# Fewer, larger transfers in a two-mixer attention layer: both heads' spills in one, doubled loads from one source pattern, one buffer for the mixed values

## The chip, the cores and the metric

The kernel runs on one NeuronCore of a Trainium2 chip, in one launch. The metric is the device time in microseconds (us) of that core, as a median over runs; lower is better. The core's engines are TensorE (PE, with its weight loads as PEld), VectorE (DVE), ScalarE (ACT), GpSimd (POOL) and SyncE (SP). In this kernel SP issues every transfer between HBM and on-chip memory, one after the other, and 16 DMA engines carry them.

## The reference

The layer normalises `x` (2048 x 1024), projects it to queries, keys, values and gates of two mixers, runs both attentions, gates and projects back.

```python
hdn = rmsnorm(x, norm_gain[i])
proj = jnp.einsum("bsd,de->bse", hdn, w_in[i])
q_a, k_a, v_a, g_a, q_b, k_b, v_b, g_b = jnp.split(proj, split_at, axis=-1)
...
o_a, _, _ = banded_attention(q_a, k_a, v_a, A_WINDOW - 1, sinks=sinks_a[i])
o_a = o_a.reshape(b, S, A_WIDTH).astype(x.dtype) * jax.nn.silu(g_a)
...
o_b = dilated_attention(q_b, k_b, v_b)
o_b = o_b.reshape(b, S, B_WIDTH).astype(x.dtype) * jax.nn.silu(g_b)

mixed = jnp.concatenate([o_a, o_b], axis=-1)
x = x + jnp.einsum("bse,ed->bsd", mixed, w_out[i])
```

Mixer A is a sliding window of 128 tokens with grouped queries and sinks. Mixer B attends under three patterns, (window, dilation) = (128, 1), (512, 4) and (2048, 16), and merges the three outputs by their softmax denominators. Both have 8 heads of 64.

## The kernel before

**Stages.** `STAGES` lists eight: four "B" stages of two heads of mixer B each, two "A" stages of four query heads each, and two "O" stages that multiply by the halves of the output matrix. A stage has four slots (`sb`, 512 tokens each), a slot two halves (`hf`, 256 tokens). All products with weights are made of three float32r products each (`mm3`, L285 to L288), where weights and `x` are split in a high and a low part. `x` is split once, in stage 0, and stored in `xd`; later stages load the stored parts (`x_load`, L180), and the O stages load the mixed values from `mx` (L185).

**Mixer B.** In slot `sb` of a B stage the windowed pattern runs from on-chip data (`units_B`). Queries, keys, the keys' low parts, values, gates, the windowed output and its row statistics are spilled to HBM under the names `qd`, `kd`, `ld`, `vd`, `gd`, `od`, `sd` (`finish`, L405 to L418; L364 for `vd`; `units_B`, L833 and L836). Four units `units_D(si, r)`, one for each residue of the token number modulo 4, then do the dilated patterns: the first when its stage ends, the other three in the slots of the next stage. For each of its two heads a unit loads queries `cq`, keys `ck`, low key parts `cl` and values `cv` (L856 to L864). Keys have 64 rows and fill 128 partitions, so `ck` and `cl` come as two copies of the same 64 rows. The unit ends in `after` (L928): it loads the windowed statistics `s1c` once a stage, works out two sets of factors, writes them to HBM as `rD` and reads them back spread over 64 partitions each (`Rb`, in `bcast`, L957). POOL multiplies by the first set (L974), then by the second (L978), and the sum goes to `mx` (L987).

**Mixer A.** `units_A` ends in the same way with reciprocals `rA` (L740), a spread load `Rb` (L750), a product on POOL (L756) and a store to `mx` (L760).

**The order of work.** The kernel's code interleaves the projection of a slot with attention pieces by a cost account (`advance`), and a scheduler then fixes each engine's order before the program runs. SP runs its transfers in that fixed order. A transfer whose data or buffer isn't ready holds up all that stand behind it. Eight semaphores are shared in turn by the transfers, so a transfer can also wait for the one eight places ahead. `Rb` has one buffer, as have `o1c` and `gc`.

Of the kernel before, what the change touches and what calls it, by code (L numbers as in the profile page):

```python
# [18 lines left out]
KC = DM // 128  # L19
# [15 lines left out]
def hybrid_layer(ctx, tc, xT, xn, x, wB, wA, wO, ng, gains, sinks, rot, masks, ident, out):  # L35
# [54 lines left out]

    rs_row = [dram([256], f"rsr{hf}") for hf in range(8)]
    xd = [dram([128, 4, 1024], f"xd{hf}") for hf in range(8)]
    mx = [dram([128, KC, 256], f"mx{hf}") for hf in range(8)]

    def bcast_row(d, lo, n, parts=128):
        return bass.AP(tensor=d.tensor, offset=d.offset + lo, ap=[[0, parts], [1, n]])
# [175 lines left out]
    def spill_tiles(si):  # L272
        if si not in spill:
            spill[si] = {
                "q": dram([2, 4, 128, 512], f"qd{si}"),
                "k": dram([2, 4, 64, 512], f"kd{si}"),
                "l": dram([4, 128, 512], f"ld{si}"),
                "v": dram([4, 4, 128, 256], f"vd{si}"),
                "g": dram([4, 128, 512], f"gd{si}"),
                "o": dram([4, 128, 512], f"od{si}"),  # L280
                "s": dram([4, 32, 4, 4, 4], f"sd{si}"),
            }
        return spill[si]

# [106 lines left out]
    def finish(si, sb, half, t1s):  # L391
        kind = STAGES[si][0]
        KK, KL = K[si, sb]
        nk = 1 if kind == "A" else 2
        if half == 0 and sb > 0:
            pk, pl = K[si, sb - 1]
            for h in range(nk):
                nc.scalar.activation(KK[:, h, :, 0, :], f32(pk[:, h, :, 4, :]), AF.Copy)
            for h in range(2):
                hs = slice(64 * h, 64 * h + 64)  # L400
                nc.scalar.activation(KL[hs, h, :, 0, :], f32(pl[hs, h, :, 4, :]), AF.Copy)
        yield from qk_transposes(si, sb, half, t1s)
        if half == 0:
            return
        if kind == "B":  # L405
            d = spill_tiles(si)
            cs = slice(sb * 128, sb * 128 + 128)
            for h in range(2):
                nc.sync.dma_start(d["q"][h][:, :, cs].rearrange("r p c -> p r c"),
                                  f32(Q[si, sb][1][:, h]))  # L410
                nc.sync.dma_start(d["k"][h][:, :, cs].rearrange("r p c -> p r c"),
                                  f32(KK[:64, h, :, 1:5, :]).rearrange("p r i u -> p r (i u)"))
            for h in range(2):
                hs = slice(64 * h, 64 * h + 64)
                nc.sync.dma_start(d["l"][:, hs, cs].rearrange("r p c -> p r c"),
                                  f32(KL[hs, h, :, 1:5, :]).rearrange("p r i u -> p r (i u)"))
            nc.sync.dma_start(d["g"][:, :, cs].rearrange("r p c -> p r c"),
                              G[si, sb][0].rearrange("p r i u -> p r (i u)"))  # L418
            pending.extend(units_B(si, sb))
            if sb == 3:  # L420
                pending.extend(units_D(si, 0))
        else:
            pending.extend(units_A(si, sb))
# [297 lines left out]
    def units_A(si, sb):  # L721
        idx = STAGES[si][1]
        sc = wk.tile([128, 2, 4, 4], F32, name="scA")
        units = []
        osum = {}

        def rows(p):
            e = wk.tile([128, 2, 4], F32, name="eA")
            hs = slice(2 * p, 2 * p + 2)
            nc.vector.tensor_tensor(e, sc[:, 0, hs], sk[:, 4 * idx + 2 * p:4 * idx + 2 * p + 2, None].to_broadcast([128, 2, 4]),  # L730
                                    op=OP.add)
            nc.scalar.activation(e, e, AF.Exp)
            nc.vector.tensor_tensor(e, e, sc[:, 1, hs], op=OP.add)
            nc.vector.reciprocal(e, e)
            pr = ps.tile([8, 128], F32, name="po", bufs=2)
            nc.tensor.transpose(pr, e.rearrange("p h i -> p (h i)"), idf)
            rr = wk.tile([16, 128], F32, name="rr")
            nc.scalar.activation(rr[:8], pr, AF.Copy)
            d = dram([8, 128], f"rA{si}_{sb}_{p}")
            nc.sync.dma_start(d, rr[:8])  # L740
            osum["d", p] = d

        def final(p):
            t = osum[p]

            def load():
                d = osum["d", p]
                rb = osum["r", p] = wk.tile([128, 512], F32, name="Rb", bufs=1)
                for a in range(2):
                    nc.sync.dma_start(rb[64 * a:64 * a + 64, :],  # L750
                                      bass.AP(tensor=d.tensor, offset=d.offset + a * 512, ap=[[0, 64], [1, 512]]))
                nc.gpsimd.tensor_tensor(t, t, G[si, sb][p].rearrange("p r i u -> p (r i u)"), op=OP.mult)

            def scale():
                mix = osum["m", p] = wk.tile([128, 512], F32, name="o1c", bufs=1)
                nc.gpsimd.tensor_tensor(cm_view(mix), cm_view(t), to_cm(osum["r", p]), op=OP.mult)  # L756

            def store():
                for a in range(2):
                    nc.sync.dma_start(mx[2 * sb + a][:, 2 * idx + p, :], osum["m", p][:, 256 * a:256 * a + 256])  # L760
                osum_free()

            late.append([[1, load], [4, scale], [2, store]])

        for p in range(2):
            units.extend(pair_units(si, sb, p, sc, osum, rows, final))
        return units
# [55 lines left out]
    def units_B(si, sb):  # L823
        sc = wk.tile([128, 4, 2, 2], F32, name="scB")
        osum = osum_tile()
        d = spill_tiles(si)
        units = []
        for h in range(2):
            def after(h=h):
                if h == 1:  # L830
                    with nc.allow_non_contiguous_dma(reason="row statistics"):
                        for r in range(4):
                            nc.sync.dma_start(d["s"][:, :, sb, r, :].rearrange("i u k -> u i k"),  # L833
                                              sc[32 * r:32 * r + 32].rearrange("p i a h -> p i (a h)"))
                    cs = slice(sb * 128, sb * 128 + 128)
                    nc.sync.dma_start(d["o"][:, :, cs].rearrange("r p c -> p r c"), osum.rearrange("p (r c) -> p r c", r=4))  # L836
                    osum_free()
            stats = ([sc[:, i, 0, h:h + 1] for i in range(4)], [sc[:, i, 1, h:h + 1] for i in range(4)])
            units.append(window_unit(si, sb, h, stats, cm_view(osum[64 * h:64 * h + 64, :]), after))
        return units  # L840


    S1 = {}

    def units_D(si, r):
        d = spill_tiles(si)
# [3 lines left out]
        def dil(h):  # L850
# [3 lines left out]
            def load():  # L854
                q = wk.tile([128, 512], F32R, name="cq")
                nc.sync.dma_start(f32(q), d["q"][h, r])  # L856
                k = wk.tile([128, 512], F32R, name="ck")
                for a in range(2):
                    nc.sync.dma_start(f32(k[64 * a:64 * a + 64, :]), d["k"][h, r])
                kl = wk.tile([128, 512], F32R, name="cl")  # L860
                for a in range(2):
                    nc.sync.dma_start(f32(kl[64 * a:64 * a + 64, :]), d["l"][r, hp:hp + 64, :])
                v = wk.tile([128, 4, 128], F32R, name="cv")
                nc.sync.dma_start(f32(v), d["v"][r][:, :, 128 * h:128 * h + 128].rearrange("t p e -> p t e"))  # L864
                s["v"], s["q"], s["k"], s["kl"] = v, q, k, kl
# [62 lines left out]
            def after():  # L928
                if h == 0:
                    return  # L930
                if (si) not in S1:
                    t = wk.tile([128, 4, 4, 4], F32, name="s1c")
                    nc.sync.dma_start(t.rearrange("p s r k -> p (s r k)"), d["s"].rearrange("i u s r k -> (i u) (s r k)"))
                    S1[si] = t
                s1 = S1[si]
                A = s1[:, :, r, :].rearrange("p t (k h) -> p k h t", k=2)
# [19 lines left out]
                o2 = c["o2"]  # L956
                def bcast(k):  # L957
                    rb = wk.tile([128, 512], F32, name="Rb", bufs=1)
                    for a in range(2):
                        nc.sync.dma_start(rb[64 * a:64 * a + 64],  # L960
                                          bass.AP(tensor=dd.tensor, offset=dd.offset + 1024 * k + a * 512, ap=[[0, 64], [1, 512]]))
                    return rb

                rbs = []
# [18 lines left out]

                def store():
                    ch = 4 + STAGES[si][1]
                    for t_ in range(4):
                        nc.sync.dma_start(mx[2 * t_ + r // 2][:, ch, 128 * (r % 2):128 * (r % 2) + 128],  # L987
                                          o2[:, 128 * t_:128 * t_ + 128])
                    osum_free()

                late.append([[1, first], [4, second], [4, third], [1, fourth], [2, store]])
# [126 lines left out]
```

## Time and profile before

| | us |
|---|---|
| median of 3 runs | 1258.38 |
| lowest, highest of them | 1250.45, 1262.69 |
| the profiled execution, its own time | 1263.84 |
| its span, first to last instruction | 1262.1 |

The profile is of one execution. Its span lacks 1.7 us of that execution's time, and that time is 5.5 us above the median. By when the stages' transfers are issued, the four B stages take roughly the first 670 us (the first about 165), the A stages the time to about 1050 us, and the O stages the rest. The loads of the dilated units run from 181 us to 817 us, their `Rb` loads from 228 us to 879 us. In the profile, issuing a transfer isn't counted as busy time; DMA shares are the mean over the 16 engines, so one engine that has more than the others is not seen in them.

### The profile page before, as it was taken

How to read it: one execution, taken by the hardware profiler on the slowest of the kernel's cores; microseconds unless marked ns; L12 is line 12 of the kernel's file. 1: busy time of each engine (PE TensorE's matmuls, PEld its weight loads, DVE VectorE, ACT ScalarE, POOL GpSimd, SP SyncE). 2: the span in 40 equal slices, each digit the busy share in tenths (PEclk: the TensorE clock that was granted, in tenths of full speed). 3: DMA queues.
4: the chain of work that ended last, by engine and by line, in shares of the span. 5: the costliest groups of instructions: out<-in, count | busy, mean ns of one | idle time of the engine just before them, and what ended most of it. 6: DMA issues, size and time to landing. Idle time of an engine off the chain costs nothing.

```text
span 1262.1 us, 24533 instructions
## 1 busy us (share of the span) xinstructions
PE 1157.7 (92%) x8040; PEld 1126.5 (89%) x8040; DVE 770.7 (61%) x2228; ACT 760.8 (60%) x2103; POOL 600.2 (48%) x720
## 2 busy tenths in 40 slices
PE   6889999979888988889797999999999999999999
PEld 5889898879887987889797989998999999999998
DVE  6856664746745665656565758878767767622321
ACT  6577755757755755757566656877766667522220
POOL 3987642544431543623534545754755465333222
PEclk9899899989989998999898999999999999999999
DMA  8978899888887797899868877857635345455652
GB/s 266 316 229 266 270 301 279 219 258 260 258 256 219 234 275 213 258 268 266 256 192 256 253 236 216 242 153 218 203 125 170 120 137 165 157 183 189 204 192 84
DMA packets 213007, 279.66 MB, mean 222 GB/s; under 512 B 36104, under 2 KB 145424, under 8 KB 212880
## 3 DMA queue, kind: packets, MB, share of 16 engines
q1 hardware_dynamic: 212880, 278.10, 71.7%
q8 instruction: 64, 1.05, 0.3%
q14 instruction: 63, 0.52, 0.1%
HBM read 206.38 MB, written 71.64 MB: 220 GB/s over the span
## 4 chain that ended last, share of the span: by engine, by line
PE 48%; DMA 22%; ACT 8%; POOL 7%; DVE 7%; SPq 4%; issue 3%; POOLq 0%; DVEq 0%; ACTq 0%
PE pj L288 33%; DMA x<-xd 4%; DMA Rb<-rD 3%; DMA stg<-in_wB 2%; PE po L923 2%; PE po L808 2%; PE pt L792 2%; PE sc L655 2%; PE po L710 2%; PE sc L656 1%; DMA cl<-ld 1%; DMA x<-in_xT 1%; DMA stg<-in_wA 1%; DMA TT<-tab 1%; DMA x<-mx 1%
## 5 line engine op out<-in xcount | busy, mean ns | idle before, releaser
L288 PE MATMUL pj<-wh,x 128*128 128x384 f32 (+1 forms) x2016 | 560.4, 333 | 7.1 <-ACT wh L104 6.7
L288 PEld LDWEIGHTS pj<-wh,x 128*128 128x128 f32 x2016 | 378.3, 193 | 10.7 <-ACT wh L104 7.0
L288 PE MATMUL pj<-wl,x 128*128 128x384 f32 (+1 forms) x1008 | 333.2, 331 | 0.0
L288 PE MATMUL pj<-x,wgh 128*128 128x256 f32 x992 | 203.3, 295 | 2.4 <-DVE V L360 2.0
L288 PEld LDWEIGHTS pj<-wl,x 128*128 128x128 f32 x1008 | 195.4, 194 | 2.1 <-DVE wl L102 0.2
L288 PEld LDWEIGHTS pj<-x,wgh 128*128 128x128 f32 x992 | 164.5, 198 | 4.4 <-ACT V L475 2.6
L639 DVE TENSOR_TENSOR ptl<-pt,pth 128x512 fp32r<-128x512 f32 (+3 forms) x232 | 141.2, 619 | 42.9 <-ACT pth L638 41.1
L288 PE MATMUL pj<-x,wgl 128*128 128x256 f32 x496 | 145.4, 293 | 0.0
L638 ACT ACTIVATE pth<-pt 128x512 fp32r<-128x512 f32 (+3 forms) x232 | 121.5, 540 | 31.3 <-PE pt L909 10.5
L193 ACT ACTIVATE x<-x 128x512 fp32r<-128x512 f32 x92 | 55.7, 625 | 132.2 <-DMA x<-mx 67.8
L288 PE MATMUL pj<-wgh,x 128*128 128x256 f32 x496 | 131.0, 285 | 0.0
L195 POOL TENSOR_TENSOR x<-x 128x512 fp32r<-128x512 f32 x58 | 76.2, 1326 | 106.0 <-ACT x L193 98.2
L523 POOL TENSOR_TENSOR Q<-ob,Q 64x256 fp32r<-64x256 f32 x96 | 72.2, 752 | 91.3 <-ACT Q L522 85.1
L888 ACT ACTIVATE P<-P,scD 128x256 f32<-128x256 f32 (+3 forms) x128 | 71.6, 560 | 44.7 <-DVE scD L887 42.6
L288 PEld LDWEIGHTS pj<-x,wgl 128*128 128x128 f32 x496 | 98.3, 198 | 0.3
L288 PEld LDWEIGHTS pj<-wgh,x 128*128 128x128 f32 x496 | 95.3, 192 | 0.0
L477 DVE TENSOR_REDUCE un<-sq 128x4 f32<-128x256 f32 (+1 forms) x96 | 42.0, 438 | 77.5 <-ACT sq L474 73.8
L887 DVE CUSTOM_DVE_ANT_0 P<-sc,mk 128x256 f32<-128x256 f32 (+3 forms) x128 | 61.4, 485 | 44.4 <-PE sc L883 40.6
L226 POOL TENSOR_TENSOR fac<-un,mhalf 128x8 f32<-128x8 f32 (+1 forms) x48 | 84.7, 1764 | 3.0
L664 ACT ACTIVATE P<-P,scB 128x256 f32<-128x256 f32 (+1 forms) x128 | 63.0, 493 | 20.7 <-DVE scB L663 20.2
L501 POOL TENSOR_TENSOR un<-un,eps 128x8 f32<-128x8 f32 (+1 forms) x48 | 10.7, 223 | 133.7 <-DVE un L477 131.7
L974 POOL TENSOR_TENSOR o1c<-o1c,Rb 128x512 f32<-128x512 f32 x16 | 21.1, 1318 | 111.7 <-DMA Rb<-rD 72.3
(171 smaller groups left out, 2735.0 us busy)
## 6 DMA issues: line engine op xcount, KB each, us to landing
x<-xd SPq DMA_DIRECT2D x160, 512.0 KB
xd<-x SPq DMA_DIRECT2D x32, 512.0 KB
x<-mx SPq DMA_DIRECT2D x32, 512.0 KB
vd<-V SPq DMA_DIRECT2D x64, 128.0 KB
qd<-qc SPq DMA_DIRECT2D x32, 256.0 KB
TT<-tab SPq DMA_DIRECT2D x32, 256.0 KB
cv<-vd SPq DMA_DIRECT2D x32, 256.0 KB
ck<-kd SPq DMA_DIRECT2D x64, 128.0 KB
```

What stands on the lines that cost most here:

```text
L193: nc.scalar.activation(h, f, AF.Copy)
L195: eng.tensor_tensor(l, f, f32(h), op=OP.subtract)
L226: nc.gpsimd.tensor_tensor(y, u, mhalf.to_broadcast([128, n]), op=OP.pow)
L288: nc.tensor.matmul(o, a, b, start=first and n == 0, stop=last and n == 2, skip_group_check=True)
L477: nc.vector.tensor_reduce(uv, sq[:, :n].rearrange("p (h d) -> p h d", d=64), axis=AX.X, op=OP.add)
L523: nc.gpsimd.tensor_tensor(o[b], src[a], f32(o[a]), op=OP.subtract)
L638: nc.scalar.activation(hi, pt, AF.Copy)
L639: nc.vector.tensor_tensor(lo, pt, f32(hi), op=OP.subtract)
L655: nc.tensor.matmul(sc[:, j, :], q[h // 2][:, h % 2, i, :], kw, start=True, stop=False)
L664: nc.scalar.activation(pd, pd, AF.Exp, bias=nb[i], scale=-1.0, accum_out=l[i])
L887: nc.vector.tensor_tensor_reduce(pd, o[:, :m], m2[:, 512 - m:], -0.125, BIG, OP.add, OP.min, nb)
L888: nc.scalar.activation(pd, pd, AF.Exp, bias=nb, scale=-1.0, accum_out=l)
```

## The change

Ten places join transfers that moved neighbouring or repeated data.

- `qd` and `kd`: both heads in one store each.
- `ck` and `cl`: one load whose source repeats the 64 rows through a leading step of 0 with a count of 2 (`twice`).
- `Rb` in both mixers: one load whose source has the two halves as a leading dimension of 2, and the repetition over 64 partitions behind it.
- `sd`: the statistics are stored as they lie in `sc`, 16 values a partition, and rearranged when they are loaded, in four loads.
- `mx`: one HBM buffer in place of eight, so that the four stores of a dilated unit, and the two of a mixer A pair, become one each.

```diff
-    mx = [dram([128, KC, 256], f"mx{hf}") for hf in range(8)]
+    mx = dram([8, 128, KC, 256], "mx")
...
-                "s": dram([4, 32, 4, 4, 4], f"sd{si}"),
+                "s": dram([4, 128, 16], f"sd{si}"),
...
-            for h in range(2):
-                nc.sync.dma_start(d["q"][h][:, :, cs].rearrange("r p c -> p r c"),
-                                  f32(Q[si, sb][1][:, h]))
-                nc.sync.dma_start(d["k"][h][:, :, cs].rearrange("r p c -> p r c"),
-                                  f32(KK[:64, h, :, 1:5, :]).rearrange("p r i u -> p r (i u)"))
+            nc.sync.dma_start(d["q"][:, :, :, cs].rearrange("h r p c -> p (h r) c"),
+                              f32(Q[si, sb][1]).rearrange("p h r c -> p (h r) c"))
+            nc.sync.dma_start(d["k"][:, :, :, cs].rearrange("h r p c -> p (h r) c"),
+                              f32(KK[:64, :, :, 1:5, :]).rearrange("p h r i u -> p (h r) (i u)"))
...
-                for a in range(2):
-                    nc.sync.dma_start(rb[64 * a:64 * a + 64, :],
-                                      bass.AP(tensor=d.tensor, offset=d.offset + a * 512, ap=[[0, 64], [1, 512]]))
+                nc.sync.dma_start(rb, bass.AP(tensor=d.tensor, offset=d.offset, ap=[[512, 2], [0, 64], [1, 512]]))
...
-                for a in range(2):
-                    nc.sync.dma_start(mx[2 * sb + a][:, 2 * idx + p, :], osum["m", p][:, 256 * a:256 * a + 256])
+                nc.sync.dma_start(mx[2 * sb:2 * sb + 2, :, 2 * idx + p, :].rearrange("a p n -> p a n"),
+                                  osum["m", p].rearrange("p (a n) -> p a n", a=2))
...
-                        for r in range(4):
-                            nc.sync.dma_start(d["s"][:, :, sb, r, :].rearrange("i u k -> u i k"),
-                                              sc[32 * r:32 * r + 32].rearrange("p i a h -> p i (a h)"))
+                        nc.sync.dma_start(d["s"][sb], sc.rearrange("p i a h -> p (i a h)"))
...
+    def twice(dst, src):
+        nc.sync.dma_start(dst, bass.AP(tensor=src.tensor, offset=src.offset, ap=[[0, 2]] + [list(x) for x in src.ap]))
...
-                for a in range(2):
-                    nc.sync.dma_start(f32(k[64 * a:64 * a + 64, :]), d["k"][h, r])
+                twice(f32(k), d["k"][h, r])
...
-                for a in range(2):
-                    nc.sync.dma_start(f32(kl[64 * a:64 * a + 64, :]), d["l"][r, hp:hp + 64, :])
+                twice(f32(kl), d["l"][r, hp:hp + 64, :])
...
-                    nc.sync.dma_start(t.rearrange("p s r k -> p (s r k)"), d["s"].rearrange("i u s r k -> (i u) (s r k)"))
+                    ds = d["s"]
+                    with nc.allow_non_contiguous_dma(reason="row statistics"):
+                        for i in range(4):
+                            nc.sync.dma_start(t[32 * i:32 * i + 32].rearrange("u s r k -> u (s r) k"),
+                                              bass.AP(tensor=ds.tensor, offset=ds.offset + 4 * i,
+                                                      ap=[[16, 32], [512, 16], [1, 4]]))
...
-                    for a in range(2):
-                        nc.sync.dma_start(rb[64 * a:64 * a + 64],
-                                          bass.AP(tensor=dd.tensor, offset=dd.offset + 1024 * k + a * 512, ap=[[0, 64], [1, 512]]))
+                    nc.sync.dma_start(rb, bass.AP(tensor=dd.tensor, offset=dd.offset + 1024 * k, ap=[[512, 2], [0, 64], [1, 512]]))
...
-                    for t_ in range(4):
-                        nc.sync.dma_start(mx[2 * t_ + r // 2][:, ch, 128 * (r % 2):128 * (r % 2) + 128],
-                                          o2[:, 128 * t_:128 * t_ + 128])
+                    nc.sync.dma_start(mx[r // 2::2, :, ch, 128 * (r % 2):128 * (r % 2) + 128].rearrange("t p n -> p t n"),
+                                      o2.rearrange("p (t n) -> p t n", t=4))
```

The scheduler makes its order anew, so transfers also change places. SP shows it best. The first place is in stage 1, from the factors of the second dilated unit of stage 0 (`rD_1`) to the loads of the next unit. A row has the line, the two names with the program's numbers, the shape and a count. Before, on SP:

```order
L960 DMA Rb<-rD_1_3047 64x512 x2
L864 DMA cv<-vd_351 128x4x128
L364 DMA vd_2097<-V 4x32x256
L833 DMA sd_2100<-scB 32x4x4 x3
L364 DMA vd_2097<-V 4x32x256
L180 DMA x<-xd_106 128x1024 x4
L455 DMA TT<-tab_6_1405 128x512
L263 DMA RB<-rsr_98 128x256
L960 DMA Rb<-rD_1_3047 64x512 x2
L856 DMA cq<-qd_348 128x512
L859 DMA ck<-kd_349 64x512 x2
L862 DMA cl<-ld_350 64x512 x2
```

The same place in the changed kernel, on SP:

```order
L960 DMA Rb<-rD_1_3011 128x1x512
L364 DMA vd_2078<-V 4x32x256
L180 DMA x<-xd_106 128x1024 x3
L841 DMA ck<-kd_342 128x1x512
L180 DMA x<-xd_106 128x1024
L854 DMA cq<-qd_341 128x512
L263 DMA RB<-rsr_98 128x256
L841 DMA cl<-ld_343 128x1x512
L960 DMA Rb<-rD_1_3011 128x1x512
L841 DMA ck<-kd_342 128x1x512
```

Each pair of `64x512` loads has become one of `128x1x512`, and the loads `ck` and `cl` of the next head now stand between the unit's two `Rb` loads.

The second place, some rows later, is the store of that unit to `mx` and the factors of the third unit. Before, on SP:

```order
L987 DMA mx_108<-osum 128x128
L987 DMA mx_110<-osum 128x128
L987 DMA mx_112<-osum 128x128
L987 DMA mx_114<-osum 128x128
L180 DMA x<-xd_107 128x1024 x2
L955 DMA rD_2_3599<-rr 16x128
L180 DMA x<-xd_107 128x1024 x2
```

The same place in the changed kernel, on SP:

```order
L985 DMA mx<-osum 128x4x128
L180 DMA x<-xd_107 128x1024 x4
L969 DMA gc<-gd_345 128x512
L263 DMA RB<-rsr_99 128x256
L416 DMA gd_2079<-G 128x4x128
L956 DMA rD_2_3546<-rr 16x128
L829 DMA sd_2081<-scB 128x16
```

Four stores have become one, as have the four of the statistics, and the factors' store `rD_2` now stands behind all four loads of `x` rather than between them.

## The prediction

> **What bounds the kernel now.** I read the page first: busy shares, the DMA rows and the chain that ended last.
>
> ```profile
> span 1262.1 us, 24533 instructions
> ...
> PE 1157.7 (92%) x8040; PEld 1126.5 (89%) x8040; DVE 770.7 (61%) x2228; ACT 760.8 (60%) x2103; POOL 600.2 (48%) x720
> ...
> DMA packets 213007, 279.66 MB, mean 222 GB/s; under 512 B 36104, under 2 KB 145424, under 8 KB 212880
> q1 hardware_dynamic: 212880, 278.10, 71.7%
> ...
> PE 48%; DMA 22%; ACT 8%; POOL 7%; DVE 7%; SPq 4%; issue 3%; POOLq 0%; DVEq 0%; ACTq 0%
> ```
>
> PE is busy 92% of the span, and the 16 DMA engines 71.7% on average. SP's issuing is only 4% of the chain, 50 us. So TensorE bounds the kernel and the DMA engines come second. The second view is the table by stretches, because shares over the whole span mix stages. Its columns are length, busy time of each engine, PE clock, DMA share, GB/s.
>
> ```profile
> 0.00:164.00 164.00, 140.37 (x857) 134.53 (x858) 111.66 (x261) 107.69 (x273) 112.42 (x146) 0.93 0.84 273
> 164.00:850.00 686.00, 616.42 (x4114) 597.46 (x4114) 434.86 (x1342) 440.39 (x1252) 309.77 (x397) 0.96 0.82 243
> 850.00:1052.00 202.00, 196.72 (x1403) 192.16 (x1402) 150.89 (x478) 142.12 (x418) 109.49 (x119) 0.99 0.50 159
> 1052.00:1262.00 210.00, 204.21 (x1673) 202.35 (x1671) 73.25 (x151) 70.59 (x162) 68.53 (x58) 0.99 0.52 171
> ...
> 520.00:580.00 60.00, 53.55 (x351) 51.58 (x351) 34.32 (x109) 35.03 (x98) 23.69 (x32) 0.97 0.93 280
> ...
> 1240.00:1262.00 22.00, 18.97 (x159) 18.77 (x157) 2.93 (x5) 1.26 (x2) 2.92 (x3) 0.99 0.13 48
> ```
>
> Between 164 and 850 us, where the dilated units load, the DMA engines are at 0.82 (0.93 in the best 60 us shown), and PE loses 70 us. There both resources are nearly full. Behind 850 us the DMA share is a half.
>
> **How a transfer is spread over the 16 engines.** The sum hangs on this. The view of the DMA issues has the name, the count and the size of one:
>
> ```profile
> vd<-V SPq DMA_DIRECT2D x64, 128.0 KB
> ...
> ck<-kd SPq DMA_DIRECT2D x64, 128.0 KB
> cl<-ld SPq DMA_DIRECT2D x64, 128.0 KB
> ...
> Rb<-rD SPq DMA_DIRECT2D x64, 128.0 KB
> ...
> Rb<-rA SPq DMA_DIRECT2D x32, 128.0 KB
> ...
> TT<-in_rot SPq DMA_DIRECT2D x16, 128.0 KB
> ...
> sd<-scB SPq DMA_DIRECT2D x64, 2.0 KB
> ...
> rA<-rr SPq DMA_DIRECT2D x16, 4.0 KB
> ...
> rsr<-RB SPq DMA_DIRECT2D x8, 1.0 KB
> s1c<-sd SPq DMA_DIRECT2D x4, 32.0 KB
> ...
> ngt<-in_ng SPq DMA_DIRECT2D x1, 4.0 KB
> sk<-in_sinks SPq DMA_DIRECT2D x1, 4.0 KB
> ```
>
> The page counts 36104 packets under 512 B. Data explains part: `sd` 64 x 128 pieces of 16 B = 8192; `TT` 16 x 512 of 256 B = 8192; `s1c` 4 x 128 of 256 B = 512; `ngt` and `sk` 256 of 32 B. 18952 remain, 15.2 for each of the 1248 issues: they must be the marks by which the engines of a transfer report its end. With 16 a transfer there would be 19968. The 1016 that lack are 64 x 12 + 16 x 8 + 8 x 15, exactly what is missing if `vd<-V` runs on 4 engines, `rA<-rr` on 8 and `rsr<-RB` on 1. Those are the sizes of their leading dimensions: `vd` is written as 4 x 32 x 256, `rA` has 8 rows, `rsr` one. So a transfer here runs on no more engines than its leading dimension counts. The chain of waits agrees: a `vd` store takes longer to land than an `Rb` load of equal bytes (start, length):
>
> ```profile
> 52.40 5.37 DMA vd<-V
> ...
> 430.00 5.41 DMA vd<-V
> ...
> 439.40 3.22 DMA Rb<-rD
> ```
>
> [...]
>
> **The change part by part.** The merged `ck`, `cl` and `Rb` loads have a source that begins with a dimension of 2 (`[0, 2]` or `[512, 2]`). By the count they run on two engines, 128 KB on each, where before 256 KB lay on 16. The other merged transfers begin with 128, 64 or 32 on both sides and stay spread.
>
> *Price of one.* 71.7% of 16 engines over 1262.1 us for 278.10 MB is 52.06 us per MB and engine, with the contention of this run. 131072 B then take 6.82 us. In the last row of the table 48 GB/s at a share of 0.13 are 23.1 GB/s an engine: 5.68 us. I take 6.25, the middle, since 14 engines will be less loaded but these two not. Spread, the same 256 KB cost an engine 0.85 us. No row has a load with a leading 2; `vd`, confined to 4, is the nearest.
>
> *The two engines' work from 164 to 850 us.* At the high price:
> - what is there, mean share 0.82 x 686: 563 us;
> - the confined `vd` stores, 48 of 64 lie here: if these fall on the same lowest engines, each gives them 32 KB rather than 8 KB, 1.28 us: +61;
> - 32 `ck`, 32 `cl`, 32 `Rb<-rD` (two of these fall behind, three `Rb<-rA` fall in, which I let cancel) no longer spread: -96 x 0.85 = -82;
> - the same 96 on two engines: +96 x 6.82 = +655.
>
> That is 1197 us of work in a stretch of 686. At the low price it is 994 (all terms by 19.2/23.1), at the middle 1096. That the same two engines serve every such transfer is an assumption that I take from `vd`: only a fixed set makes the work pile up (second rival). How full can they be kept? SP is in order and at most eight transfers share its semaphores. In each unit SP waits for the landing of `rD` before `Rb`, and for POOL's product before the second `Rb`, while little else is queued. The stretch itself shows 0.82, its best 60 us 0.93; I take 0.875. 1096/0.875 = 1253, so **+567 us**. PE's 616 us lie inside it.
>
> *From 850 us on.* 13 to 16 `Rb<-rA` add at most 16 x 5.4 = 86 us on two engines that have 101 us in 202: it fits. Later landings, with SP and POOL in order behind them, cost between 0 and 86 us; POOL already waits there (second row below) while PE is busy 196.72 of 202 us, so I take **+10**.
>
> ```profile
> POOL o1c L974 <- DMA Rb<-rD: 72.3, 10, 11.6
> ...
> POOL o1c L756 <- DMA Rb<-rA: 66.3, 13, 8.7
> ...
> DVE mn L939 <- DMA s1c<-sd: 10.9, 3, 5.3
> ```
>
> *What is saved.* Issues go from 1248 to 1004: `mx` 48 and 16, `ck`, `cl`, `Rb<-rD` 32 each, `Rb<-rA` 16, `sd` 48, `qd` and `kd` 16 each, less 12 more `s1c`. One takes (ns, least/median/greatest):
>
> ```profile
> L859 SPq DMA_DIRECT2D ck<-kd x64: 444/500/1881, 181.4 to 814.3; - x64
> L960 SPq DMA_DIRECT2D Rb<-rD x64: 444/535/1373, 227.6 to 879.4; - x64
> L987 SPq DMA_DIRECT2D mx<-osum x64: 319/423/1822, 247.1 to 892.7; - x64
> L833 SPq DMA_DIRECT2D sd<-scB x64: 302/430/1537, 88.0 to 728.3; - x64
> ```
>
> At about 0.48 us that frees 117 us of SP, nearly all beside other work: SP's part of the chain is 50 us, and 244/1248 of it is **-10**. Fewer transfers also mean that each of the eight semaphores stands for more bytes (the waits below); where the two engines are the bound, a place ahead buys nothing, so 0.
>
> ```profile
> SPq L862 <- DMA x<-xd: 14.4, 13, 1.8
> ...
> SPq L833 <- DMA x<-xd: 11.5, 11, 1.7
> ```
>
> *At nothing:* `qd`, `kd`, `mx` keep bytes, pieces and 16 engines. For the statistics 8192 pieces of 16 B move from stores to loads; before, DVE waited 10.9 us in all for `s1c`, and four loads rather than one bound it between a gain of that and a loss of some 4 x 4 us. The cover is that four loads a stage are all there are. In one `mx`, loads of a half wait only for its own stores, as far as the order of waits in the program shows.
>
> Sum: 1263.8 + 567 + 10 - 10 = 1831 on the profiled execution, which lies 5.5 us above the median: about **1825 us**.
>
> **Rivals.**
>
> *The other side: spread after all (faster).* If only the leading dimension of the on-chip side or of the written side counts (it is 128), all stay on 16 engines. Then the gain stands alone: 10 us of issuing, and of the SP waits behind earlier transfers up to 26 us (the two rows above). 1258 less 10 to 36: about 1235 us. For it: `vd` is narrow on the written side, and the new loads on the read side only, which no row tests. Against it: `rA` and `rsr` are narrow on both sides. It decides as soon as those loads post 16 marks each. [...]
>
> *Two engines, but other ones each time.* Then the mean load stays as it is and only each landing comes 5.4 us later. On the chain stand about 20 such loads (`Rb` 3.4%, `cl` 1.5%, in pieces of 3 to 7 us):
>
> ```profile
> by line: PE pj L288 33.3%; DMA x<-xd 3.6%; issue 3.4%; DMA Rb<-rD 3.4%; DMA stg<-in_wB 2.0%; PE po L923 1.9%; PE po L808 1.6%; PE pt L792 1.5%; PE sc L655 1.5%; PE po L710 1.5%; PE sc L656 1.5%; DMA cl<-ld 1.5%; DMA x<-in_xT 1.4%; DMA stg<-
> ```
>
> 20 x 5.4 gives 1258 + 108 = 1366 us. For it: no view names an engine, so a set that turns from transfer to transfer is not excluded. Against: the count fits sets that follow from the shape alone, without a memory of the transfer before; that is why it gets little. [...]
>
> **How the numbers follow.** Two engines, always the same: 0.84. Other engines each time: 0.08. Spread: 0.08. The first case's bounds: low price and a fill of 0.93, 994/0.93 = 1069, +383, 1263.8 + 383 - 16 = 1632; high price and 0.82, 1197/0.82 = 1460, +774, with 40 for the A stages 2070. The range 1600 to 2070 leaves out the two rivals and a little of the first case. A measurement of this kernel can tell about 1% from no change. Slower by over 1%: 0.84 + 0.08, 0.92. Spread splits: 0.05 faster by over 1% (below 1246), 0.03 within.
>
> **What would show it.** Marks: with `ck`, `cl`, `Rb` on two engines, packets under 512 B become 1004 x 16 - 1016 - 112 x 14 = 13480 marks and 18688 small pieces of data (`sd` now 2048 of 64 B, `s1c` 8192 of 16 B), 32168; spread, 33736. If the engines pile up, the mean DMA share falls to about 563/1253 = 0.45 in the stretch of the dilated units while the stretch grows past 1000 us, PE waits there for `x`, `ck` and `cl`, PE's busy total stays near 1158 us, and a merged load takes 8 us or more to land. The forecast is wrong if that stretch stays under 800 us, or if the share rises instead.

## The result and the profile after

| | before | after |
|---|---|---|
| median, us | 1260.54 (4 runs) | 1664.53 (4 runs) |
| lowest, highest | 1250.45, 1263.57 | 1661.57, 1666.79 |
| ratio of the means | | 1.3222, 95% interval 1.3142 to 1.3302 |

The change costs 404 us. The page of the changed kernel, its profiled execution 1664.86 us long:

```profile
span 1663.0 us, 24214 instructions
...
PE 1226.0 (74%) x8040; PEld 1184.0 (71%) x8040; DVE 757.0 (46%) x2228; ACT 761.0 (46%) x2103; POOL 594.1 (36%) x720
...
DMA packets 209069, 279.62 MB, mean 168 GB/s; under 512 B 32168, under 2 KB 141488, under 8 KB 208944
q1 hardware_dynamic: 208944, 278.07, 53.4%
...
PE 35%; DMA 33%; issue 11%; POOL 7%; ACT 6%; DVE 4%; SPq 3%; POOLq 0%; ACTq 0%; DVEq 0%
```

The same bytes move as before (278.07 MB against 278.10) and the mean share of the DMA engines falls from 71.7% to 53.4%, yet DMA's part of the chain rises from 22% to 33%. A mean can't show that. The number that can is the 32168 packets under 512 B, exactly the count forecast for `ck`, `cl` and `Rb` on two engines each.

The table by stretches is cut at 164 us, then at 1207 us, after as many matmuls as the same stretch had before (4116 against 4114), and at 1462 us. The last cut is not at the count of a cut before, so the last two rows are compared as a sum:

```profile
164.00:1207.00 1043.00, 673.97 (x4116) 645.80 (x4115) 429.11 (x1348) 442.18 (x1257) 305.35 (x397) 0.80 0.52 160
1207.00:1462.00 255.00, 221.18 (x1541) 213.14 (x1540) 160.76 (x496) 155.41 (x451) 117.83 (x128) 0.95 0.43 138
1462.00:1663.00 201.00, 188.42 (x1524) 185.94 (x1522) 58.31 (x124) 55.02 (x122) 59.63 (x49) 0.98 0.51 162
```

The stretch of the dilated units grew from 686 to 1043 us, +357, while its DMA share fell from 0.82 to 0.52. From its end to the end of the span there were 412 us and are now 456: +44. The waits show who pays (engine, line and releaser; us in all, times, longest):

```profile
POOL o1c L973 <- DMA Rb<-rD: 236.6, 15, 27.0
...
PE sc L654 <- POOL Q L522: 150.2, 15, 26.7
...
POOL o1c L753 <- DMA Rb<-rA: 114.8, 13, 14.5
...
PE sc L878 <- DMA cq<-qd: 60.6, 7, 18.2
...
PE sc L879 <- DMA cl<-ld: 46.1, 10, 5.9
```

POOL's wait for `Rb` went from 72.3 to 236.6 us. POOL works in the program's fixed order, and PE waits 150 us for the product `Q` that POOL makes behind the one with `Rb` (L522; L523 before). Before the change the largest such row was 20 us in all:

```profile
PE sc L655 <- POOL Q L523: 19.9, 7, 7.7
```

The chain that ended last in the changed kernel has such a place (start, length). POOL multiplies by `Rb` as soon as it lands, then makes `Q` and `klz`; PE, idle for 18.9 us, goes on at 343.4 when it has them:

```profile
321.27 19.07 DMA Rb<-rD
340.48 1.27 POOL osum L977
341.81 0.72 POOL Q L522
342.61 0.73 POOL klz L541
```

PE also waits for `cq`, which by the count of marks is spread over 16 engines, but which SP issues among the confined loads. The one issued at 237.84, 1.27 us after a confined `ck`, is waited for until 249.37, 11.5 us later (PE sits idle for 3.74 of them). The one `cq` in the chain of the kernel before landed after 4.89 us.

One place shows the two engines alone. First SP's rows (start, length of the issue), then PE's, then the table for 248 to 252 us:

```profile
236.57 0.51 SPq L841 DMA_DIRECT2D ck<-kd  x1
...
240.03 0.50 SPq L841 DMA_DIRECT2D cl<-ld  x1
...
245.52 2.58 SPq L841 DMA_DIRECT2D ck<-kd  x1
```

```profile
254.70 0.58 PE L879 MATMUL sc<-cl,cq 128*128 128x256 f32 x1 [4.87 <-DMA cl<-ld]
```

```profile
248.00:252.00 4.00, 0.47 (x2) 0.22 (x2) 0.00 (x0) 0.27 (x1) 0.04 (x1) 0.80 0.13 50
252.00:256.00 4.00, 1.30 (x5) 1.30 (x6) 0.68 (x3) 0.35 (x2) 0.00 (x0) 0.50 0.34 103
```

The `cl` issued at 240.03 lands only at 254.7, where PE's wait for it ends, and a `ck` issued at 245.52 is queued too. Between 248 and 252 us the share is 0.13, two engines of 16, at 50 GB/s. A second pair of engines for the second load would have made it 0.25. So it is the same pair, and it moves 25 GB/s an engine: 5.2 us for the 128 KB that a load puts on each.

### The profile page after: what moved, and what is told of

It is laid out like the page before. It is cut to its first block, busy times and chain, and to the rows that moved or that the text cites. A ratio compares the mean times of both kernels' runs of the same rounds, so it can differ in the third digit from the quotient of the medians.

```text
span 1663.0 us, 24214 instructions
## 1 busy us (share of the span) xinstructions
PE 1226.0 (74%) x8040; PEld 1184.0 (71%) x8040; DVE 757.0 (46%) x2228; ACT 761.0 (46%) x2103; POOL 594.1 (36%) x720
## 2 busy tenths in 40 slices
DMA packets 209069, 279.62 MB, mean 168 GB/s; under 512 B 32168, under 2 KB 141488, under 8 KB 208944
## 3 DMA queue, kind: packets, MB, share of 16 engines
q1 hardware_dynamic: 208944, 278.07, 53.4%
## 4 chain that ended last, share of the span: by engine, by line
PE 35%; DMA 33%; issue 11%; POOL 7%; ACT 6%; DVE 4%; SPq 3%; POOLq 0%; ACTq 0%; DVEq 0%
PE pj L288 24%; DMA Rb<-rD 7%; DMA cl<-ld 6%; DMA Rb<-rA 3%; DMA stg<-in_wB 3%; DMA cq<-qd 3%; DMA stg<-in_wA 2%; DMA rD<-rr 2%; DMA x<-in_xT 2%; PE po L709 2%; DMA x<-mx 1%; DMA x<-xd 1%; PE sc L655 1%; POOL fac L226 1%; PE sc L654 1%
## 5 line engine op out<-in xcount | busy, mean ns | idle before, releaser
L288 PE MATMUL pj<-wh,x 128*128 128x384 f32 (+1 forms) x2016 | 571.8, 340 | 12.5 <-ACT wh L104 6.2
L288 PEld LDWEIGHTS pj<-wh,x 128*128 128x128 f32 x2016 | 390.3, 199 | 18.1 <-ACT wh L104 6.4
L288 PE MATMUL pj<-wl,x 128*128 128x384 f32 (+1 forms) x1008 | 342.3, 340 | 0.0
L654 PE MATMUL sc<-KK,Q 128*128 128x256 f32 x192 | 61.3, 343 | 151.0 <-POOL Q L522 150.2
L654 PEld LDWEIGHTS sc<-KK,Q 128*128 128x128 f32 x192 | 41.9, 223 | 155.5 <-POOL Q L522 155.1
L883 DVE CUSTOM_DVE_ANT_0 P<-sc,mk 128x128 f32<-128x128 f32 (+3 forms) x128 | 62.0, 487 | 190.5 <-PE sc L879 177.9
L884 ACT ACTIVATE P<-P,scD 128x128 f32<-128x128 f32 (+3 forms) x128 | 71.5, 559 | 131.9 <-DVE scD L883 124.9
L401 ACT ACTIVATE klz<-klz 64x128 fp32r<-64x128 f32 x36 | 11.1, 307 | 221.7 <-POOL klz L541 169.1
L878 PE MATMUL sc<-ck,cq 128*128 128x256 f32 (+2 forms) x128 | 49.2, 389 | 81.2 <-DMA cq<-qd 60.6
L973 POOL TENSOR_TENSOR o1c<-o1c,Rb 128x512 f32<-128x512 f32 x16 | 20.6, 1285 | 245.5 <-DMA Rb<-rD 236.6
L655 PE MATMUL sc<-klz,Q 128*128 128x256 f32 x192 | 59.9, 329 | 62.6 <-POOL klz L565 41.0
```

What stands on the lines that cost most here:

```text
L288: nc.tensor.matmul(o, a, b, start=first and n == 0, stop=last and n == 2, skip_group_check=True)
L654: nc.tensor.matmul(sc[:, j, :], q[h // 2][:, h % 2, i, :], kw, start=True, stop=False)
L655: nc.tensor.matmul(sc[:, j, :], q[h // 2][:, h % 2, i, :], lw, start=False, stop=True)
L878: nc.tensor.matmul(o, q[:, qs], k[:, :n], start=True, stop=False)
L883: nc.vector.tensor_tensor_reduce(pd, o[:, :m], m2[:, 512 - m:], -0.125, BIG, OP.add, OP.min, nb)
L884: nc.scalar.activation(pd, pd, AF.Exp, bias=nb, scale=-1.0, accum_out=l)
```

## The experiments

Two theories were put against each other. *Pile-up*: every confined load (one that runs on fewer than 16 engines) goes to the same engines, these become the bound, and all spread transfers queue behind them. *Later landing*: only who waits for a confined load loses. A third was that another part of the change, or the new order, costs the time. Medians are in us; each ratio is of means, to the kernel before in the same runs, with its 95% interval.

**Only the leading dimension changed.** Each instruction keeps its place on every engine; only the sources of the merged loads differ (the `ap` alone is shown). They read other rows, so these forms show the time only:

```diff
-ap=[[0, 2]] + [list(x) for x in src.ap]
+ap=[[2 * 512, 16], [512, 8], [1, 512]]
...
-ap=[[512, 2], [0, 64], [1, 512]]
+ap=[[32, 16], [0, 8], [1, 512]]
```

> The changed kernel with the leading dimension of the merged ck, cl and Rb loads' sources made 16 instead of 2: the same number, size and place of every transfer, but other rows are read, so the keys of the dilated units and the spread factors are not the reference's. Pile-up on a fixed pair of engines (the theory): with the leading 2 gone, each of those loads costs an engine 0.7 us rather than 5.4, the stretch is PE's again, and the time is 1245 us (1230 to 1265), at or a little under the kernel before. Later landings only: 1260 us. New order, merging or the single mx as the cause: it stays at 1665 us.

Measured: 1232.68, ratio 0.9826 (0.9775 to 0.9876). The whole loss is gone, with the same transfers in the same order on every engine.

> The same with a leading dimension of 8; the same rows are wrong in the same way. Pile-up: eight engines get 16 x 2 KB of each such load, 1.35 us; work of the fullest engine in the dilated stretch about 474 + 58 + 96 x 1.35 = 660 us, less than PE needs there, so about 1260 us (1240 to 1290): nearly all comes back. Later landings in proportion to the transfer's length: 0.67 of 4.7 us more than spread, a seventh of the 404 us: about 1318 us. Order or merging: 1665 us.

Measured: 1294.93, ratio 1.0305 (1.0256 to 1.0355), above the band for pile-up and between the two theories.

> The same with a leading dimension of 4; the same rows are wrong in the same way. Pile-up: four engines get 32 x 2 KB of each, 2.7 us; the fullest engine has 474 + 58 + 96 x 2.7 = 790 us of work where the kernel before took 686: about 1380 us (1340 to 1430). Later landings: 2.0 of 4.7 us more than spread, 1434 us. Order or merging: 1665 us.

Measured: 1437.95, ratio 1.1452 (1.1399 to 1.1505), outside the band for pile-up and almost the 1434 of later landing. The completion marks in the three pages follow the leading dimension, 16, 8 and 4 in this order:

```profile
DMA packets 210637, 279.63 MB, mean 228 GB/s; under 512 B 33736, under 2 KB 143056, under 8 KB 210512
```

```profile
DMA packets 209741, 279.62 MB, mean 216 GB/s; under 512 B 32840, under 2 KB 142160, under 8 KB 209616
```

```profile
DMA packets 209293, 279.62 MB, mean 195 GB/s; under 512 B 32392, under 2 KB 141712, under 8 KB 209168
```

33736 - 32840 = 112 x 8, 33736 - 32392 = 112 x 12, and 33736 - 32168 = 112 x 14: the 112 merged loads post as many marks as their leading dimension counts. But the times grow almost in proportion to the length of one load, which is how later landing was described. So the degree alone doesn't decide, and the next runs were made for that.

What failed for pile-up at 8 is its condition, that the work of the fullest engine costs nothing while it is less than PE needs. The stretch of the dilated units at a leading 16, 8 and 4:

```profile
158.00:814.00 656.00, 607.48 (x4114) 585.72 (x4113) 443.54 (x1344) 439.07 (x1255) 311.12 (x398) 0.98 0.84 256
160.00:874.00 714.00, 626.77 (x4119) 601.78 (x4117) 434.25 (x1345) 440.72 (x1255) 309.14 (x398) 0.95 0.78 235
161.00:998.00 837.00, 646.92 (x4120) 620.09 (x4119) 428.37 (x1340) 440.12 (x1254) 307.34 (x397) 0.88 0.67 200
```

An estimate from the mean share, with 5.2 us for a load on two engines and in proportion for more, makes the fullest engines 0.84, 0.87 and 0.89 full, or 0.91, 0.93 and 0.95 if the `vd` stores lie on them too. At a leading 8 they are thus less than full, and the time rises all the same.

**Only those loads in the kernel before.** The spills, statistics and `mx` stay as they were.

> The kernel before with only the ck, cl and Rb loads merged (source leading with 2); spills, statistics and mx stay as before. Pile-up: the whole loss is here, 1640 to 1700 us. Other parts of the change (statistics in 16-byte pieces, one mx, larger spills) as the cause: near 1260 us, or between.

Measured: 1659.76, ratio 1.3231 (1.3167 to 1.3295). The loss is in these 112 loads; the 5 us between this and the changed kernel are within the intervals.

**Confined transfers that nobody waits for.** To the form with leading 16, 64 stores of a gate tile to unused HBM were added beside the gate spills of the B stages. The four runs differ in the leading dimension of these stores alone, on the written side; the source tile has 128 partitions. Shown is a leading 2:

```diff
+            for m in range(4):
+                z = dram([192, 512], f"z{si}_{sb}_{m}")
+                nc.sync.dma_start(bass.AP(tensor=z.tensor, offset=z.offset, ap=[[72 * 512, 2], [512, 64], [1, 512]]),
+                                  G[si, sb][0].rearrange("p r i u -> p (r i u)"))
```

> The spread form (leading dimension 16, 1233 us; its key rows and factors are not the reference's) with 64 stores more of 256 KB each, four beside every gate spill of the B stages, that nothing reads; they lead with 16. Each gives every engine 0.7 us, 44 us in all on engines some 0.85 to 0.9 full: 1250 to 1285 us by both theories. It is the other half of the next run.

Measured: 1238.78, ratio 0.9861 (0.982 to 0.9903): 6 us more than without the stores, which the intervals don't tell from nothing, and below what was expected. Evenly spread, 16.8 MB more were nearly free.

> The same kernel and order, but the 64 stores that nothing reads lead with 2. Pile-up on a fixed pair: the pair gets 64 x 5.4 = 346 us of work on top of what is about 0.9 full already, and all spread transfers queue behind it, so the time rises by 230 to 330 us over the run before, to 1490 to 1600 us, though nobody waits for these stores. Later landings of awaited loads as the cause: nobody waits, so it stays within 30 us of the run before.

Measured: 1497.64, ratio 1.1937 (1.1882 to 1.1991): 259 us over the run before, 4.0 us a store. The same bytes, and no engine reads what they write. The packets under 512 B are 33864 here and 34760 with a leading 16, 64 x 2 and 64 x 16 more than the 33736 without the stores, so a leading 2 on the written side alone confined these too. Of the two theories only pile-up gives this; a set of engines that turned from transfer to transfer would have left it near the run before. Whether the others lose more on the pair itself or at SP, which is held at these stores (1786 ns in the median for an issue, 572 with a leading 16; last section), was not separated.

> The kernel with 64 stores that nothing reads (its key rows and factors are not the reference's), the stores leading with 4. The awaited loads cost 205 us for 112 at a leading 4, 1.83 us each. If piling up is the whole cost at every degree, these stores cost as much each: 117 us over the form that leads with 16 (1239), about 1355 us (1325 to 1385). If at a mild degree the later landing of loads that are waited for is the larger part, far less: 1250 to 1300 us.

Measured: 1358.62, ratio 1.0798 (1.0755 to 1.084): 120 us over the spread stores, where pile-up gave 117.

> The same, leading with 8. The awaited loads cost 62 us for 112, 0.55 us each. Piling up alone: 35 us over the form that leads with 16, about 1274 us. Later landing of awaited loads: within 12 us of it, 1235 to 1250 us.

Measured: 1285.99, ratio 1.0238 (1.0195 to 1.028): 47 us over them, where pile-up gave 35 and later landing under 12. The 117 and 35 us are not from the sum of pile-up but from what an awaited load had cost at the same degree. So at every degree stores that nobody waits for cost about what the awaited loads cost. That the confined transfer itself is waited for isn't needed; that it adds something for awaited loads isn't excluded.

| leading dimension | a 256 KB transfer on each of its engines, over spread, us | 112 awaited loads over `lead16`, us each | 64 stores over `extra16`, us each |
|---|---|---|---|
| 8 | 0.65 | 0.56 | 0.74 |
| 4 | 2.0 | 1.83 | 1.87 |
| 2 | 4.6 | 3.9 (changed kernel) | 4.0 |

The second column takes 5.2 us for a leading 2 and less in proportion to the bytes that an engine gets, minus the 0.65 us of a leading 16; the others are differences of medians above divided by 112 or 64.

**The two kinds of load apart.** In the kernel before, first only `Rb`, then only `ck` and `cl` were merged, with the edits of the change.

> The kernel before with only the Rb loads merged (48 confined loads). Pile-up: 32 of them lie in the dilated stretch, 32 x 5.4 = 173 us more on the pair less 27, on top of engines that are 0.9 full: about +150 us there, and little from the 16 of mixer A, where the engines are half full: about 1400 us (1350 to 1450). If the round trip of the factors alone carried the loss (POOL's waits for Rb), most of the 404 us would be here: over 1550 us.

Measured: 1422.65, ratio 1.1327 (1.1265 to 1.139): 168 us for 48 loads, 3.5 us each, as pile-up has it; the round trip of the factors alone would have been over 1550.

> The kernel before with only the ck and cl loads merged (64 confined loads, all in the dilated stretch). Pile-up: 64 x 5.4 = 346 us more on the pair less 54: about +260 us, 1515 us (1460 to 1570); together with the run before the two parts add up to about the whole 404 us. If these loads were hidden because they are issued ahead: within 30 us of the kernel before.

Measured: 1495.34, ratio 1.19 (1.1821 to 1.1979): 241 us for 64 loads, 3.8 us each. That is pile-up's band again, and loads issued ahead are not hidden. The two add up to 409 us, where the change lost 404. The stretches, cut at the same matmuls, first of `Rb` alone, then of `ck` and `cl` alone:

```profile
162.00:960.00 798.00, 637.99 (x4118) 613.93 (x4117) 426.87 (x1341) 439.18 (x1255) 305.27 (x397) 0.90 0.70 209
960.00:1421.00 461.00, 418.26 (x3069) 407.57 (x3067) 226.41 (x627) 211.65 (x576) 178.03 (x177) 0.95 0.45 147
```

```profile
163.00:1076.00 913.00, 664.69 (x4114) 636.00 (x4112) 430.46 (x1339) 439.04 (x1251) 306.55 (x397) 0.85 0.59 184
1076.00:1492.00 416.00, 402.74 (x3072) 396.85 (x3071) 222.86 (x631) 212.88 (x580) 178.67 (x177) 0.98 0.50 163
```

Behind the dilated units the kernel before has 412 us. `Rb` alone makes it 461, `ck` and `cl` alone 416: the 44 us that the change loses there come with the `Rb` loads, most of them mixer A's `Rb<-rA`, though the engines are only half full on average.

**The change without these loads.**

```diff
-                twice(f32(k), d["k"][h, r])
+                for a in range(2):
+                    nc.sync.dma_start(f32(k[64 * a:64 * a + 64, :]), d["k"][h, r])
```

and likewise for `cl` and both `Rb`.

> The changed kernel with only the ck, cl and Rb loads in two parts again, as before (64 partitions each, 16 engines); spills of both heads, statistics and one mx stay merged. Pile-up: 1235 to 1255 us, a gain of 0 to 2% on the kernel before. If another part of the change costs time: over 1265 us.

Measured: 1251.01, ratio 0.9967 (0.9937 to 0.9998). 132 fewer issues gain 0.3%, 4 us, with the interval's end almost at 1.

**One load of 128 rows that leads with 128.** Keys and their low parts are spilled from all 128 partitions, so that `ck` and `cl` are plain loads; `Rb` stays in two parts.

```diff
-                "k": dram([2, 4, 64, 512], f"kd{si}"),
-                "l": dram([4, 128, 512], f"ld{si}"),
+                "k": dram([2, 4, 128, 512], f"kd{si}"),
+                "l": dram([2, 4, 128, 512], f"ld{si}"),
...
-                twice(f32(k), d["k"][h, r])
+                nc.sync.dma_start(f32(k), d["k"][h, r])
...
```

> As the run before, but keys and low key parts are spilled on all 128 partitions (the low parts with the zeros that stand in the other half, so the product of the queries' low parts with them is left out), and ck and cl are one plain load of 128 rows each: 64 loads fewer, 8.4 MB more to write, half of it zeros. Pile-up: 16 engines everywhere, so about the spread form's 1233 us, 1225 to 1250; the extra bytes are 8.4 x 52 / 16... 0.5 MB an engine, 27 us of engine time over four stages, against some 5 us of saved issuing. If a load of 128 rows in one were slow in itself, not by its engines: far over 1260 us.

Measured: 1212.18, ratio 0.9646 (0.9615 to 0.9676), below the expected band and the fastest of all. Its page:

```profile
span 1212.6 us, 24265 instructions
...
PE 1146.1 (95%) x8040; PEld 1115.9 (92%) x8040; DVE 779.3 (64%) x2228; ACT 761.0 (63%) x2103; POOL 603.0 (50%) x720
...
q1 hardware_dynamic: 227408, 286.47, 73.6%
```

It moves 8.4 MB more than before at a higher DMA share (73.6%), and PE is busy 95%. How much of its gain over the run before it (39 us) is from 80 fewer issues, and how much from the order that the scheduler made for it, was not taken apart.

## Why the prediction was right

**The engines of a transfer.** Right, and exact: the count of packets under 512 B came out at 32168. The three other leading dimensions bear it out for a narrow source as well, which no row before had shown: 32392 at 4, 32840 at 8, 33736 at 16. For a narrow written side the 33864 of `extra2` do.

**Always the same engines.** Assumed then; shown now by the stretch at 0.13 with two loads queued, and by the 259 us of stores that nobody waits for. Which two of the 16 they are, no run shows. Nor does one show that the `vd` stores fall on them, or that they are the lowest ones, as the +61 us in the sum supposes; shown are 4 marks a store by the count, and 5.37 and 5.41 us to land for the two on the chain before.

**The price of a load, 6.25 us.** Too high: 5.2 us by the 50 GB/s at a share of 0.13. The forecast's lower end, 5.68, was itself still above it.

**The pair's work and how full it can be kept.** These two terms of the sum were mis-sized, and both made the stretch too long. The work was put at 1096 us. With 5.2 us a load it follows from the stretch after: 0.52 x 1043 = 542 us mean, of which 96 x 5.2 x 2/16 = 62 are the loads'; 480 are spread work, `vd` adds 48 x 0.98 = 47 if its stores fall on these engines too, the loads 96 x 5.2 = 499, in all 1026 us. Within it a part cancelled by luck: the loads were some 100 us too high, the spread work some 40 too low, because the busy time that the profile shows there had been scaled with the price. The stretch was 1043 us, so by this account the pair was full to 0.98 where 0.875 was taken, between the shares 0.82 and 0.93. That SP always has something queued for a pair that is far behind would explain it; no run shows it apart. 1253 us were forecast for the stretch and 1043 came, 210 us less: 80 by the work (1026/0.875 = 1173), 130 by the fill. The 34 us more behind it and the 10 that were not saved leave 166, the distance from the sum of 1831 to the profiled 1664.86. So the mechanism was right, and the forecast was a tenth too high by these two sizes. The ends of its range add up to 1631 and 2062 us by its own terms, where it has 1632 and 2070; that changes nothing.

**From 850 us on, +10.** Mis-sized: +44, within the bounds given (0 to 86), and with the `Rb` loads, not with `ck` and `cl`. That the engines had room for these loads was the reason for a small term; half full on average, they still cost time.

**What is saved, -10.** The sign held where the loads stay spread: 0.3% without merged loads, 1.7% with them at a leading 16. In the changed kernel itself no saving is seen: 1664.5 against 1659.8 us with the loads alone merged.

**At nothing.** Statistics, larger spills and one `mx` cost nothing that the runs show; `rest` has all of them and is 0.3% faster.

**The signs.** The stretch passed 1000 us, the share in it fell (to 0.52, where 0.45 was named), and a `cl` took 14.7 us to land, over the 8 named. Two signs came otherwise. PE's longest wait in total isn't for `x`, `ck` or `cl` but for POOL's product behind `Rb` (150.2 us), then for `cq` (60.6) and only then for `cl` (46.1). And PE's busy total rose to 1226 us, where 1158 were to stay, at a granted clock of 0.80 in the stretch, 0.96 before (last section).

**The rivals.** "Spread after all" was priced at 1235 us; the run that makes the loads spread gave 1233, so the price was right and its condition false. "Other engines each time" was priced at 1366 and is excluded as told above.

## What to carry to other kernels

Before merging transfers, look at the leading dimension of both sides, and behind the change at the count of packets under 512 B. Here a source that led with 2, as a repeat of 2 or two halves do, ran on two engines (14 marks fewer for each of 112 loads), the same ones by the share of 0.13 with two loads queued and by the 259 us of stores that nobody waits for. Each microsecond that this added there cost about 0.9 us of the whole (0.85 to 1.15 in the table above), where the engines had been about 0.8 full (0.82 in the stretch before, 0.84 at a leading 16). The mean DMA share hid it: it fell from 71.7% to 53.4% while the time rose by a third. Storing the data so that one plain load of 128 rows brings it, with 8.4 MB more moved, turned the loss of 32% into a gain of 3.5%.

## What the runs showed of the hardware that wasn't expected

SP was held at the issue itself. In the runs with the added stores the issue of one (ns, least/median/greatest) took, leading with 2 and then with 16:

```profile
L418 SPq DMA_DIRECT2D z<-G x64: 483/1786/6152, 48.8 to 911.5; - x64
```

```profile
L418 SPq DMA_DIRECT2D z<-G x64: 517/572/2275, 50.4 to 669.2; - x64
```

Three times as long in the median (1786 ns against 572), with the same bytes from the same tile. Issues of transfers that have nothing to do with the confined ones' data grew too: in the changed kernel that of an `x` load took up to 7.0 us; in the kernel before the longest took 1.3 us (before, then after).

```profile
L180 SPq DMA_DIRECT2D x<-xd x160: 315/395/1286, 139.0 to 1013.6; - x160
L180 SPq DMA_DIRECT2D x<-xd x160: 319/424/7049, 133.3 to 1396.2; - x160
```

TensorE also lost speed. The granted clock of the stretch fell from 0.96 to 0.80, in the rows above to 0.50 for 252 to 256 us, right behind 4 us in which PE was busy for 0.47, and the same 8040 matmuls took 1226 us rather than 1158. What lowered the clock, no run shows.

The confinement of the `vd` stores to four engines, which both kernels have by the count of marks (64 x 12 missing from 16 a store), was not tried otherwise; what it costs stays open.
